# Two decoder blocks on one core: four heads' scores ahead of the expert gathers, eight ids first, and tiles moved by 32 bytes

## The chip, the core and the metric

The kernel runs on one core of a Trainium2 chip. The metric is device time in microseconds; the time before is 1990.11 us, the median of three runs (1988.2 to 1990.91). Engines are named as in the profile: PE (TensorE; PEld is its weight load), DVE (VectorE), ACT (ScalarE), POOL (GpSimd), SP (SyncE, which here only issues DMAs).

## The reference

256 tokens of width 1024 pass through two layers of a first model (each: feed-forward, mixer, feed-forward, with norms) and one layer of a second (a state-space branch and an mLSTM branch). The last part retrieves experts: for each token and each of 8 heads, 16 out of 16384 rows of two tables.

```python
q = (xb @ w_q).reshape(256, 8, 2, 128)
s = einsum('thid,hikd->thik', q, keys)            # 128 scores per half
sv, si = top_k(s, 16)                             # per half
cand = sv[..., 0, :, None] + sv[..., 1, None, :]  # 256 pairs
cs, ci = top_k(cand, 16)                          # 16 expert ids
gate = softmax(cs)
act = gelu(einsum('td,thkd->thk', xb, u_tab[eidx]))
y = einsum('thk,thkd->td', gate * act, v_tab[eidx])
out = rmsnorm(x + y, final_norm)
```

## The kernel before

**Dense part.** Every large product is computed in three passes with values split into a high and a low part (`split`, `split_scaled`): `whi`/`wlo` for the weights, `xp` (and `hh`/`hl`, `yh`/`yl`, ...) for the activations. `weights` loads a block of 1 MB (or 704 KB) into `raw` over SP's queue; `split_piece` makes `whi` on ACT and `wlo` on DVE. `acc` then issues, for each 128 rows, three matmuls of 256 columns with the weights stationary and the activations moving (L170, L171, L172); `accn` (the values `v` of the two attention mixers) has the roles the other way round (L180 to L182). The four feed-forward layers hold 4 x (11 x 2 x 48 + 8 x 66) = 6336 such matmuls; in all 9384 matmuls of 256 columns are built, 336 of them for the heads 1 to 7 of the last part.

**Tiles.** Tiles lie in pools one behind the other: `const`, `keep`, `act` and `tmp` from the bottom up, the dense weights (`wp`) from the top down. A tile takes a multiple of 32 bytes of each partition. All activations begin 32 bytes past a multiple of 64, and so do the weights. `eps2` (L52, one float, 32 bytes) lies in `const`, below nearly everything.

**Expert part** (`peer`). `score` projects a head (48 matmuls `pq`, as above), copies it to `pqT`, and multiplies by the keys (`psc`); from head 1 on the scores are copied to SBUF (`psb`). `route` turns 128 + 128 scores per token into 16 ids and gates, all on DVE: `top16` twice, 256 pairs (`cand`), `top16` again, then two one-hot products (`oh`) that look the ids up; the last is L1150. `tokens` makes the transposed tokens `hn` and the normed `xn`. `expert` (L1246) gathers one row of 8 KB per token (u and v side by side, 1 MB in all) with an indirect DMA from POOL. For every gathered tile DVE computes a dot product (L1264); two at a time ACT makes the gelu and a diagonal matrix `dg`, and PE adds `dg` times v into four banks `acc` (L1276). Only then is the tile `uv` free; there are 7 + 3 of them (`LATE`, `MORE`). There are 256 gathers: 8 heads x 2 halves of the tokens x 16. While head h is gathered, head h + 1 is scored and routed.

A scheduler orders each engine's instructions; `issue_after` holds an instruction behind another one. POOL issues the gathers in the program's order, SP its loads likewise.

**The end.** DVE adds the last expert into `hn`, adds `acc` (L1286), ACT sums the squares (L1287), DVE scales by the norm and the gain `gf` (L1293), and SP stores.

Of the kernel before, what the change touches and what calls it, by code (L numbers as in the profile page):

```python
# [17 lines left out]
T = 256  # L18
# [5 lines left out]
LATE, MORE = 7, 3  # L24
# [7 lines left out]
class Net:  # L32
    def __init__(self, ctx, tc, a):
        self.tc, self.nc, self.a, self.ctx = tc, tc.nc, a, ctx
        nc = self.nc
        self.const = ctx.enter_context(tc.tile_pool(name="const", bufs=1))
        self.keep = ctx.enter_context(tc.tile_pool(name="keep", bufs=1))
        self.dense = ExitStack()
        self.act = self.dense.enter_context(tc.tile_pool(name="act", bufs=1))
        self.tmp = self.dense.enter_context(tc.tile_pool(name="tmp", bufs=2))  # L40
        self.weighed = ExitStack()
        self.wp = self.weighed.enter_context(tc.tile_pool(name="wp", bufs=3, side="right"))
        self.dram = ctx.enter_context(tc.tile_pool(name="dram", bufs=1, space=bass.MemoryType.DRAM))
# [1080 lines left out]
    def route(self, s, r, out):  # L1124

        nc, v = self.nc, self.nc.vector
        pk = self.late.tile([128, 18, 16], F32, tag="route", name="route", bufs=6)
        two = lambda i: pk[:, i:i + 2, :]
        sv, si, ab, abf, sif, e = two(0), two(2).bitcast(U32), two(4).bitcast(U32), two(6), two(8), two(10)
        cs, ci, ids, gate = pk[:, 12, :], pk[:, 13, :].bitcast(U32), pk[:, 14, :].bitcast(I32), pk[:, 15, :]  # L1130
        out.append((ids, gate, pk[:, 16, :], pk[:, 17, :]))
        wide = lambda name: self.late.tile([128, 16, 16], F32, tag="wide", name=name, bufs=4)
        sc = wide("rsc").rearrange("p a b -> p (a b)")
        for j in range(2):
            yield from self.top16(sv[:, j], si[:, j], s[:, j], sc[:, 0:128])
        cand = wide("cand")
        yield v.tensor_tensor(cand, sv[:, 0].unsqueeze(2).to_broadcast([128, 16, 16]),
                              sv[:, 1].unsqueeze(1).to_broadcast([128, 16, 16]), OP.add)
        yield from self.top16(cs, ci, cand.rearrange("p a b -> p (a b)"), sc)
        v.tensor_scalar(ab[:, 0], ci, 4, None, op0=OP.logical_shift_right)  # L1140
        yield v.tensor_scalar(ab[:, 1], ci, 15, None, op0=OP.bitwise_and)
        v.tensor_copy(abf, ab)
        yield v.tensor_copy(sif, si)
        for j in range(2):
            oh = wide("oh")
            yield v.tensor_tensor(oh, abf[:, j].unsqueeze(2).to_broadcast([128, 16, 16]),
                                  self.iota16.unsqueeze(1).to_broadcast([128, 16, 16]), OP.is_equal)
            yield v.tensor_tensor(oh, oh, sif[:, j].unsqueeze(1).to_broadcast([128, 16, 16]), OP.mult)
            yield v.tensor_reduce(e[:, j], oh, axis=mybir.AxisListType.X, op=OP.add)
        self.routed = v.scalar_tensor_tensor(ids, e[:, 0], 128.0, e[:, 1], op0=OP.mult, op1=OP.add).ins  # L1150
# [7 lines left out]
    def peer(self, st, x, out):  # L1158
# [6 lines left out]
        for t, n in ((gn, "peer_g"), (gf, "out_g")):  # L1165
            nc.sync.dma_start(t, a[n].partition_broadcast(128))
# [4 lines left out]
        def tokens(i):  # L1171
# [6 lines left out]
            nc.vector.scalar_tensor_tensor(xn[i], hn[i], self.rcol(st)[:, i:i + 1], gn, op0=OP.mult, op1=OP.mult)  # L1178

        def score(hd, got):  # L1180
# [16 lines left out]
            if hd > 0:  # L1197
                kept = late.tile([128, 2, 256], F32, tag="psb", name="psb", bufs=2)
                for i in range(2):
                    nc.scalar.activation(kept[:, i], banks[i], AF.Copy)  # L1200
                banks = [kept[:, i] for i in range(2)]
            got += banks
            self.latest = (copied,)
            yield

        def routes(hd, out):

            s = []
            yield from score(hd, s)
            for i in range(2):  # L1210
                steps = self.route(s[i].rearrange("p (j k) -> p j k", j=2), lambda: self.rcol(st)[:, i:i + 1], out)
# [4 lines left out]
                with ExitStack() as ctx:  # L1216
# [3 lines left out]
                    while self.routed is first:  # L1220
                        next(steps)
                with self.tc.issue_after(self.routed):
                    for _ in steps:
                        pass
                if i == 0:
                    ids = self.routed
                with self.tc.issue_after(ids):
                    tokens(i)

        rt = []  # L1230
# [19 lines left out]
        for hd in range(8):  # L1250
            here, rt = rt, []
            ahead = routes(hd + 1, rt) if hd < 7 else iter(())
            for i in range(2):
# [3 lines left out]
                for k0, k1 in zip(cuts, cuts[1:]):  # L1257
                    uv = {}
                    for k in range(k0, k1):
# [4 lines left out]
                        nc.vector.scalar_tensor_tensor(u, u, 1.0, xn[i], op0=OP.mult, op1=OP.mult, accum_out=dots[:, k:k + 1])  # L1264
# [3 lines left out]
                    for k in range(k0, k1):  # L1268
                        vt = uv[k][:, D:]
                        if hd == 7 and k >= 13 and k % 2 == 1:  # L1270
                            nc.vector.scalar_tensor_tensor(hn[i], vt, w[:, k:k + 1], hn[i], op0=OP.mult, op1=OP.add)
                            continue
                        dg = late.tile([128, 128], F32, tag="dg", name="dg", bufs=8)
                        nc.scalar.activation(dg, self.ident, AF.Copy, scale=w[:, k:k + 1])  # L1274
                        for b in range(2):
                            nc.tensor.matmul(acc[i][b], dg, vt[:, b * 512:(b + 1) * 512], start=hd == 0 and k == 0,  # L1276
# [4 lines left out]
        for i in range(2):  # L1281
            z = late.tile([128, 4], F32, tag="z4", name="z4", bufs=2)
            sq = late.tile([128, 512], F32, tag="osq", name="osq", bufs=2)
# [7 lines left out]
            for b in range(2):  # L1291
                c = slice(b * 512, (b + 1) * 512)
                nc.vector.scalar_tensor_tensor(hn[i][:, c], hn[i][:, c], z[:, 3:4], gf[:, c], op0=OP.mult, op1=OP.mult)  # L1293
                nc.sync.dma_start(out[i * 128:(i + 1) * 128, c], hn[i][:, c])
# [130 lines left out]
```

## Time and profile before

| | |
|---|---|
| median of three runs | 1990.11 us |
| the profiled execution | 1995.88 us |
| its span, first to last instruction | 1994.1 us |
| PE busy | 1806.1 us (91%) |
| DVE busy | 1351.1 us (68%) |
| ACT busy | 852.6 us (43%) |
| bytes read from HBM | 488.8 MB, of them 268.45 MB by the gathers |

A matmul's busy time overlaps that of the next, so its cost in a stream is the distance from one start to the next (the pitch). The span falls into two parts: to about 1300 us the dense part, then the expert part.

### The profile page before, as it was taken

The page shows a single profiled execution, that of the slowest core. Times are in us where ns is not written, and L with a number is a line of the kernel's source. Part 1 is how long each engine was busy: PE and PEld are TensorE (multiplying, and loading weights), DVE is VectorE, ACT ScalarE, POOL GpSimd, SP SyncE. Part 2 cuts the span into 40 slices and gives each one's busy share as a digit, 9 for nine tenths or more (in the row PEclk, how much of TensorE's full clock was granted, in tenths as well). Part 3 has the DMA queues.
Part 4 walks back from the last instruction along what each step waited for, and adds up shares of the span by engine and source line. Part 5 has one row for each costly group of instructions (what it writes and reads, how often), then busy time and mean ns, then how long its engine had stood idle before and what let it go on. Part 6 is the DMA issues. An engine that isn't in the chain of part 4 may idle for free.

```text
span 1994.1 us, 31435 instructions
## 1 busy us (share of the span) xinstructions
PE 1806.1 (91%) x12097; PEld 1457.0 (73%) x12097; DVE 1351.1 (68%) x2490; ACT 852.6 (43%) x1391; POOL 605.8 (30%) x831
## 2 busy tenths in 40 slices
PE   8999899999999999999999999979988787777776
PEld 7999899999999998899997699855643333222222
DVE  6765677875675567675676376789866766665556
ACT  5544645554544466554444465444422322221112
POOL 5002212141240100200235851244344344443342
PEclk9999999999999999999999799979999899999998
DMA  5556425555554553264464125479899999999996
GB/s 209 195 175 206 149 88 184 197 188 188 195 180 163 194 179 128 98 239 169 155 223 144 43 88 177 175 304 421 360 409 421 420 422 421 421 421 421 422 421 285
DMA packets 81022, 493.30 MB, mean 247 GB/s; under 512 B 14389, under 2 KB 16693, under 8 KB 28393
## 3 DMA queue, kind: packets, MB, share of 16 engines
q0 software_dynamic: 36864, 268.45, 32.5%
q1 hardware_dynamic: 36616, 219.79, 31.6%
q10 hardware_dynamic: 7392, 3.05, 0.8%
q8 instruction: 96, 1.57, 0.3%
q14 instruction: 54, 0.43, 0.1%
HBM read 488.80 MB, written 2.13 MB: 246 GB/s over the span
## 4 chain that ended last, share of the span: by engine, by line
PE 55%; DMA 19%; DVE 14%; issue 5%; ACT 4%; POOL 3%; another core or an unknown queue 0%; DVEq 0%; SPq 0%; POOLq 0%; ACTq 0%
DMA uv<-in_peer_uv,route 15%; DVE uv L1264 4%; PE up L172 4%; PE up L171 4%; PE gate L172 4%; PE gate L170 4%; PE up L170 4%; PE gate L171 4%; PE o L170 4%; PE o L171 3%; PE o L172 3%; PE acc L1276 3%; DVE wlo L186 2%; ACT whi L185 2%; PE ip L172 1%
## 5 line engine op out<-in xcount | busy, mean ns | idle before, releaser
L186 DVE TENSOR_TENSOR wlo<-raw,whi 128x1024 fp32r<-128x1024 f32 (+3 forms) x451 | 512.3, 1151 | 192.2 <-ACT whi L185 180.9
L1276 PE MATMUL acc<-uv,dg 128*128 128x512 f32 x1008 | 484.1, 629 | 131.2 <-ACT dg L1274 131.1
L185 ACT ACTIVATE whi<-raw 128x1024 fp32r<-128x1024 f32 (+3 forms) x451 | 424.7, 964 | 345.7 <-PE gate L171 75.4
L1276 PEld LDWEIGHTS acc<-uv,dg 128*128 128x128 f32 x1008 | 191.8, 199 | 410.1 <-ACT dg L1274 208.0
L1264 DVE SCALAR_TENSOR_TENSOR uv<-uv,xn 128x1024 f32<-128x1024 f32 x256 | 311.3, 1221 | 149.5 <-DMA uv<-in_peer_uv,route 144.2
L1246 POOL DMA_INDIRECT uv<-in_peer_uv,route x256 | 282.1, 1102 | 387.1 <-PE acc L1276 237.3
L170 PE MATMUL gate<-xp,whi 128*128 128x256 f32 x704 | 199.0, 283 | 7.1 <-ACT whi L185 7.1
L172 PE MATMUL gate<-xp,wlo 128*128 128x256 f32 x704 | 197.9, 281 | 3.7 <-DVE wlo L186 3.7
L171 PE MATMUL gate<-xp,whi 128*128 128x256 f32 x704 | 197.4, 280 | 0.0
L172 PE MATMUL o<-hh,wlo 128*128 128x256 f32 x704 | 194.4, 276 | 0.5 <-DVE wlo L186 0.5
L172 PE MATMUL up<-xp,wlo 128*128 128x256 f32 x704 | 194.6, 276 | 0.0
L170 PE MATMUL up<-xp,whi 128*128 128x256 f32 x704 | 194.6, 276 | 0.0
L171 PE MATMUL up<-xp,whi 128*128 128x256 f32 x704 | 194.6, 276 | 0.0
L170 PE MATMUL o<-hh,whi 128*128 128x256 f32 x704 | 194.4, 276 | 0.0
L171 PE MATMUL o<-hl,whi 128*128 128x256 f32 x704 | 194.3, 276 | 0.0
L1266 ACT ACTIVATE route<-route 128x2 f32<-128x2 f32 x129 | 26.2, 203 | 387.7 <-DVE uv L1264 386.6
L170 PEld LDWEIGHTS gate<-xp,whi 128*128 128x128 f32 x704 | 135.0, 192 | 8.1 <-ACT whi L185 7.4
L172 PEld LDWEIGHTS gate<-xp,wlo 128*128 128x128 f32 x704 | 134.5, 191 | 5.0 <-DVE wlo L186 5.0
L171 PEld LDWEIGHTS gate<-xp,whi 128*128 128x128 f32 x704 | 134.9, 192 | 0.2
L172 PEld LDWEIGHTS o<-hh,wlo 128*128 128x128 f32 x704 | 132.2, 188 | 0.7 <-DVE wlo L186 0.7
L170 PEld LDWEIGHTS up<-xp,whi 128*128 128x128 f32 x704 | 132.4, 188 | 0.0
L170 PEld LDWEIGHTS o<-hh,whi 128*128 128x128 f32 x704 | 132.2, 188 | 0.1
(437 smaller groups left out, 3754.4 us busy)
## 6 DMA issues: line engine op xcount, KB each, us to landing
raw<-in_ffn_w_up SPq DMA_DIRECT2D x44, 1024.0 KB, 4.8
raw<-in_ffn_w_down SPq DMA_DIRECT2D x64, 704.0 KB, 4.2
raw<-in_ffn_w_gate SPq DMA_DIRECT2D x43, 1024.0 KB, 4.8
raw<-in_w_in SPq DMA_DIRECT2D x18, 1024.0 KB, 4.8
raw<-in_gla_in SPq DMA_DIRECT2D x12, 1024.0 KB, 4.8
raw<-in_sb_in SPq DMA_DIRECT2D x12, 1024.0 KB, 4.8
raw<-in_peer_q SPq DMA_DIRECT2D x8, 1024.0 KB, 8.9
raw<-in_gla_w_out SPq DMA_DIRECT2D x4, 1024.0 KB, 5.5
```

The costliest lines, as they stand in the source:

```text
L170: nc.tensor.matmul(ps, hi, xh, start=start and n == 0, stop=False)
L171: nc.tensor.matmul(ps, hi, xl, start=False, stop=False)
L172: nc.tensor.matmul(ps, lo, xh, start=False, stop=stop and n == len(steps) - 1)
L185: return (self.nc.scalar.activation(h, src, AF.Copy).ins, self.nc.vector.tensor_tensor(l, src, h.bitcast(F32), OP.subtract).ins)
L186: self.nc.vector.tensor_tensor(l, src, h.bitcast(F32), OP.subtract).ins)
L1246: nc.gpsimd.indirect_dma_start(out=t, out_offset=None, in_=a["peer_uv"], in_offset=bass.IndirectOffsetOnAxis(ap=ids[:, k:k + 1], axis=0))
L1264: nc.vector.scalar_tensor_tensor(u, u, 1.0, xn[i], op0=OP.mult, op1=OP.mult, accum_out=dots[:, k:k + 1])
L1266: gelu = nc.scalar.activation(w[:, ks], dots[:, ks], AF.Gelu_apprx_tanh).ins
L1276: nc.tensor.matmul(acc[i][b], dg, vt[:, b * 512:(b + 1) * 512], start=hd == 0 and k == 0, stop=hd == 7 and k == 14)
```

## The change

1. `eps2` is taken from a tile of nine floats, which takes 64 bytes where one float took 32: every tile of `keep`, `act`, `tmp` and most of `const` moves up by 32 bytes and now begins at a multiple of 64. The weights `whi` and `wlo` stay 32 bytes off. The gathered tiles stay 32 bytes off as well.
2. Heads 1 to 4 are scored right behind head 0 (`AHEAD = 4`), ahead of the first gather's use. The gain `gf` is loaded behind them.
3. For head 0 and the first half of the tokens, `route` takes the first 8 ids from the best 8 of each half (64 pairs; no pair outside them can be among the best 8), and the other 8 ids after that.
4. `rcol_alone` takes the column of norms from the square root's output without the row's reciprocal.
5. There are 8 + 3 gathered tiles, 6 `dg` tiles in place of 8, 14 rows in a `route` tile in place of 18.
6. `hn` enters `acc` by four matmuls with the identity. The last expert of each half adds onto `acc` directly; the 14th goes through PE like the others. At the end `gf` is multiplied in before the norm is known, and ACT scales one half.

```diff
-LATE, MORE = 7, 3
+LATE, MORE = 8, 3
+AHEAD = 4
...
-        self.eps2 = c.tile([128, 1], F32, name="eps2")
+        self.eps2 = c.tile([128, 9], F32, name="eps2")[:, 0:1]
...
+    def rcol_alone(self, st):
+
+        nc = self.nc
+        if st.rc is None:
+            r = self.keep.tile([128, T], F32, tag="rs", name="rs", bufs=1)
+            st.sqrt = nc.scalar.activation(r, self.mean_squares(st.squares), AF.Sqrt, bias=self.eps).ins
+            p = self.bank([128, 2])
+            for i in range(2):
+                nc.tensor.matmul(p[:, i:i + 1], r[0:1, i * 128:(i + 1) * 128], self.one1, start=True, stop=True)
+            st.rc = self.const.tile([128, 2], F32, name="rcol")
+            nc.vector.reciprocal(st.rc, p)
+        return st.rc
...
+        if soon:
+            for _ in range(2):
+                for j in range(2):
+                    yield next(steps[j])
+            low = slice(0, 8)
+            v.tensor_copy(sif[:, :, low], si[:, :, low])
+            some = self.wide("some", 8, 8)
+            yield v.tensor_tensor(some, *pairs(8), OP.add)
+            yield v.max(cs[:, low], flat(some))
+            cl = self.late.tile([128, 8], U32, tag="cl", name="cl", bufs=1)
+            yield v.max_index(cl, cs[:, low], flat(some))
+            yield from self.chosen(e[:, :, low], cl, sif[:, :, low], 8, 8)
+            self.routed = join(low)
+            yield
+            done = 8
...
-                kept = late.tile([128, 2, 256], F32, tag="psb", name="psb", bufs=2)
+                kept = late.tile([128, 2, 256], F32, tag="psb", name="psb", bufs=AHEAD)
...
-            self.latest = (copied,)
+            self.latest = (copied,) if hd > AHEAD else (self.ids0,) if hd else self.latest
...
+        for hd in range(1, 1 + AHEAD):
+            scored[hd] = []
+            for _ in score(hd, scored[hd]):
+                pass
+        nc.sync.dma_start(gf, a["out_g"].partition_broadcast(128))
...
+        for i in range(2):
+            for b in range(2):
+                nc.tensor.matmul(acc[i][b], self.ident, hn[i][:, b * 512:(b + 1) * 512], start=True, stop=False)
...
-                        nc.vector.scalar_tensor_tensor(u, u, 1.0, xn[i], op0=OP.mult, op1=OP.mult, accum_out=dots[:, k:k + 1])
+                        with self.tc.issue_after(self.rest0):
+                            nc.vector.scalar_tensor_tensor(u, u, 1.0, xn[i], op0=OP.mult, op1=OP.mult, accum_out=dots[:, k:k + 1])
...
-                        if hd == 7 and k >= 13 and k % 2 == 1:
-                            nc.vector.scalar_tensor_tensor(hn[i], vt, w[:, k:k + 1], hn[i], op0=OP.mult, op1=OP.add)
+                        if hd == 7 and k == 15:
+                            for b in range(2):
+                                c = slice(b * 512, (b + 1) * 512)
+                                nc.vector.scalar_tensor_tensor(hn[i][:, c], vt[:, c], w[:, k:k + 1], acc[i][b], op0=OP.mult, op1=OP.add)
...
-                nc.vector.tensor_tensor(hn[i][:, c], hn[i][:, c], acc[i][b], OP.add)
-                nc.scalar.activation(sq, hn[i][:, c], AF.Square, accum_out=z[:, b:b + 1])
+                nc.scalar.activation(xn[i][:, c], hn[i][:, c], AF.Square, accum_out=z[:, b:b + 1])
+            nc.vector.tensor_tensor(gn, hn[i], gf, OP.mult)
```

How the instructions move is shown at three places. Up to head 0's scores every engine but SP, ACT and DVE (two splits of head 1) has the same instructions in the same order.

On DVE, the end of the way from head 0's scores to the first ids, before (`cand` holds the 256 pairs, `rsc` the same without the best eight, `oh` the one-hot products, `wlo` is a weight split of head 1; the last row makes the ids of 16 experts):

```order
L1119 MAX_INDEX route<-route,cand 128x8
L1120 MATCH_REPLACE rsc<-route,cand 128x256
L1121 MAX route<-rsc 128x8
L1122 MAX_INDEX route<-route,rsc 128x8
L1140 TENSOR_SCALAR route<-route 128x16
L1141 TENSOR_SCALAR route<-route 128x16
L1142 CAST route<-route 128x32
L1146 TENSOR_TENSOR oh<-route,iota_14954 128x256 x2
L1148 TENSOR_TENSOR oh<-oh,route 128x256 x2
L1149 TENSOR_REDUCE route<-oh 128x16 x2
L186 TENSOR_TENSOR wlo<-raw,whi 128x1024
L1150 SCALAR_TENSOR_TENSOR route<-route 128x16
```

and now the whole way from the 64 pairs (`some`) on; the row L1169 makes the ids of 8 experts:

```order
L1179 TENSOR_TENSOR some<-route 128x64
L1177 CAST route<-route 128x2x8
L1180 MAX route<-some 128x8
L1182 MAX_INDEX cl<-route,some 128x8
L1143 TENSOR_SCALAR ab<-cl 128x8
L1144 TENSOR_SCALAR ab<-cl 128x8
L1145 CAST abf<-ab 128x2x8
L1148 TENSOR_TENSOR oh<-abf,iota_14953 128x64 x2
L1150 TENSOR_TENSOR oh<-oh,route 128x64 x2
L1151 TENSOR_REDUCE route<-oh 128x8 x2
L1169 SCALAR_TENSOR_TENSOR route<-route 128x8
L1134 MATCH_REPLACE rsc<-route,psc 128x128
```

The second best eight of each half and of the pairs, and head 1's split, no longer stand ahead of the first ids.

On SP, at the same place, before (`peer_q` is a head's weights, `keys` the sub-keys, `gn` and `gf` two gains):

```order
L152 DMA raw<-in_w_out 128x2048 x4
L152 DMA raw<-in_peer_q 128x2048
L1163 DMA keys<-in_peer_keys 128x2048
L1166 DMA gn<-in_peer_g 128x1024
L1166 DMA gf<-in_out_g 128x1024
L152 DMA raw<-in_peer_q 128x2048 x7
```

and now:

```order
L153 DMA raw<-in_w_out 128x2048 x4
L153 DMA raw<-in_peer_q 128x2048 x3
L1213 DMA keys<-in_peer_keys 128x2048
L1215 DMA gn<-in_peer_g 128x1024
L153 DMA raw<-in_peer_q 128x2048
L1292 DMA gf<-in_out_g 128x1024
L153 DMA raw<-in_peer_q 128x2048 x4
```

The keys, which head 0's scores need, stand behind the weights of heads 1 and 2.

On PE, around the first use of a gathered tile, now (`acc<-hn` is the identity product, `acc<-uv` the gathered tiles):

```order
L171 MATMUL pq<-xp,whi 128x256
L172 MATMUL pq<-xp,whi 128x256
L173 MATMUL pq<-xp,wlo 128x256
L1244 MATMUL psc<-keys,pqT 128x128 x4
L1299 MATMUL acc<-hn_14955,ident 128x512 x2
L1299 MATMUL acc<-hn_14956,ident 128x512 x2
L1341 MATMUL acc<-uv,dg 128x512 x32
```

The first `acc<-uv` stands behind all matmuls of heads 1 to 4; before it stood behind head 1 and the first two matmuls of head 2.

## Rows read from the trace of the kernel before

**Rows 1.** The page: busy time, share and instructions of PE.
```profile
PE 1806.1 (91%) x12097; PEld 1457.0 (73%) x12097; DVE 1351.1 (68%) x2490; ACT 852.6 (43%) x1391; POOL 605.8 (30%) x831
```
**Rows 2.** Windows of 100 us to 1300: engines' busy time (instructions), granted clock, DMA.
```profile
100.00:200.00 100.00, 99.79 (x879) 99.53 (x878) 61.05 (x77) 45.71 (x61) 11.58 (x16) 1.00 0.56 190
...
sum 1300.00, PE 1266.98 PEld 1210.04 DVE 867.56 ACT 658.33 POOL 323.76; mean PE 97.46 PEld 93.08 DVE 66.74 ACT 50.64 POOL 24.90
```
**Rows 3.** Timeline of PE, attention projection: start, duration, engine, line, instruction.
```profile
749.18 0.28 PE L171 MATMUL qk<-xp,whi 128*128 128x256 f32 x1
...
750.88 0.28 PE L171 MATMUL qk<-xp,whi 128*128 128x256 f32 x1
```
**Rows 4.** Windows of the expert part: PE, PEld, DVE, ACT, POOL, clock, DMA share, GB/s.
```profile
1300.00:1310.00 10.00, 1.84 (x13) 1.24 (x11) 9.26 (x39) 3.54 (x4) 0.00 (x0) 0.70 0.03 9
...
1400.00:1410.00 10.00, 9.12 (x33) 5.10 (x34) 9.97 (x29) 6.82 (x13) 3.81 (x3) 1.00 0.76 282
...
1440.00:1460.00 20.00, 19.24 (x73) 10.95 (x72) 11.39 (x23) 4.54 (x16) 8.55 (x7) 1.00 0.85 329
...
1800.00:1900.00 100.00, 73.55 (x161) 28.53 (x160) 52.10 (x101) 18.00 (x60) 38.33 (x40) 1.00 1.01 421
```
**Rows 5.** Timeline of POOL: the first gather issued, and the eleventh.
```profile
1310.23 1.16 POOL L1246 DMA_INDIRECT uv<-in_peer_uv,route  x1 [13.84 <-DVE route L1150]
...
1332.92 0.95 POOL L1246 DMA_INDIRECT uv<-in_peer_uv,route  x1 [8.53 <-PE acc L1276]
```
**Rows 6.** The chain that ended last, its end: start, duration, what.
```profile
1964.58 18.73 DMA uv<-in_peer_uv,route
...
1983.40 1.25 DVE uv L1264 x2
...
1985.10 1.29 DVE hn L1271
...
1989.44 0.75 DVE hn L1293
```
**Rows 7.** Timeline of PE, values of the first mixer (activations stationary).
```profile
247.55 0.28 PE L180 MATMUL v<-whi,xp 128*128 128x256 f32 x1
...
248.49 0.28 PE L182 MATMUL v<-whi,xp 128*128 128x256 f32 x1
```
**Rows 8.** Timeline of PE, second model's input projection, 272 columns.
```profile
1046.96 0.29 PE L170 MATMUL ip<-xp,whi 128*128 128x272 f32 x1
...
1048.98 0.29 PE L171 MATMUL ip<-xp,whi 128*128 128x272 f32 x1
```
**Rows 9.** Timeline of PE, merged: plain float32 matmuls of 128 and 512 columns.
```profile
267.69 1.39 PE L371 MATMUL sc<-qt,kt 128*128 128x128 f32 x11
...
1455.85 14.00 PE L1276 MATMUL acc<-uv,dg 128*128 128x512 f32 x32
```
**Rows 10.** Timeline of DVE: head 0's scores to the first ids.
```profile
1300.40 0.30 DVE L1118 MAX8 route<-psc 128x8 f32<-128x128 f32 x1 [4.61 <-PE psc L1195]
...
1304.69 0.41 DVE L1120 MATCH_REPLACE8 rsc<-route,cand 128x256 f32<-128x256 f32 x1
...
1308.64 1.21 DVE L186 TENSOR_TENSOR wlo<-raw,whi 128x1024 fp32r<-128x1024 f32 x1
1309.77 0.17 DVE L1150 SCALAR_TENSOR_TENSOR route<-route 128x16 int32<-128x16 f32 x1
```
**Rows 11.** Timeline of ACT: a split of head 0, and its copy.
```profile
1285.11 1.04 ACT L185 ACTIVATE whi<-raw 128x1024 fp32r<-128x1024 f32 x1
...
1299.21 0.66 ACT L1190 ACTIVATE pqT<-pq 128x256 f32<-128x256 f32 x2 [3.94 <-PE pq L172]
```
**Rows 12.** Timeline of SP: two DMA issues.
```profile
1279.32 0.42 SPq L1163 DMA_DIRECT2D keys<-in_peer_keys  x1
...
1294.57 18.79 SPq L152 DMA_DIRECT2D raw<-in_peer_q  x2
```
**Rows 13.** Timeline of DVE: head 0's second weight split.
```profile
1288.79 1.23 DVE L186 TENSOR_TENSOR wlo<-raw,whi 128x1024 fp32r<-128x1024 f32 x1 [0.62 <-ACT whi L185]
```

More of the change, by code (lines that the diff above doesn't have):

```diff
@@ L1122, in top16, with chosen @@
         yield v.max_index(idx[:, 8:16], vals[:, 8:16], scratch)
-    def route(self, s, r, out):
+    def chosen(self, e, ci, si, n, m):
+        v = self.nc.vector
+        ab = self.late.tile([128, 2, 16], U32, tag="ab", name="ab", bufs=2)[:, :, :n]
+        abf = self.late.tile([128, 2, 16], F32, tag="abf", name="abf", bufs=2)[:, :, :n]
+        v.tensor_scalar(ab[:, 0], ci, m.bit_length() - 1, None, op0=OP.logical_shift_right)
+        yield v.tensor_scalar(ab[:, 1], ci, m - 1, None, op0=OP.bitwise_and)
+        yield v.tensor_copy(abf, ab)
+        for j in range(2):
+            oh = self.wide("oh", n, m)
+            yield v.tensor_tensor(oh, abf[:, j].unsqueeze(2).to_broadcast([128, n, m]),
+                                  self.iota16[:, :m].unsqueeze(1).to_broadcast([128, n, m]), OP.is_equal)
+            yield v.tensor_tensor(oh, oh, si[:, j].unsqueeze(1).to_broadcast([128, n, m]), OP.mult)
+            yield v.tensor_reduce(e[:, j], oh, axis=mybir.AxisListType.X, op=OP.add)
@@ L1126, in route, with wide @@
+    def wide(self, name, n=16, m=16):
+        t = self.late.tile([128, 256], F32, tag="wide", name=name, bufs=4)[:, :n * m]
+        return t.rearrange("p (a b) -> p a b", a=n)
+    def route(self, s, r, out, soon=False):
         nc, v = self.nc, self.nc.vector
-        pk = self.late.tile([128, 18, 16], F32, tag="route", name="route", bufs=6)
+        pk = self.late.tile([128, 14, 16], F32, tag="route", name="route", bufs=6)
         two = lambda i: pk[:, i:i + 2, :]
-        sv, si, ab, abf, sif, e = two(0), two(2).bitcast(U32), two(4).bitcast(U32), two(6), two(8), two(10)
@@ L1130, in route @@
[L1130 to L1133, printed above, removed]
-        for j in range(2):
[L1135 to L1142, printed above, removed]
-        yield v.tensor_copy(sif, si)
[L1144 to L1149, printed above, removed]
@@ L1150, in route @@
-        self.routed = v.scalar_tensor_tensor(ids, e[:, 0], 128.0, e[:, 1], op0=OP.mult, op1=OP.add).ins
+        sv, si, sif, e = two(0), two(2).bitcast(U32), two(4), two(6)
+        cs, ci, ids, gate = pk[:, 8, :], pk[:, 9, :].bitcast(U32), pk[:, 10, :].bitcast(I32), pk[:, 11, :]
+        out.append((ids, gate, pk[:, 12, :], pk[:, 13, :]))
+        flat = lambda t: t.rearrange("p a b -> p (a b)")
+        sc = flat(self.wide("rsc"))
+        pairs = lambda n: (sv[:, 0, :n].unsqueeze(2).to_broadcast([128, n, n]), sv[:, 1, :n].unsqueeze(1).to_broadcast([128, n, n]))
@@ new lines, in route @@
+        join = lambda n: v.scalar_tensor_tensor(ids[:, n], e[:, 0, n], 128.0, e[:, 1, n], op0=OP.mult, op1=OP.add).ins
+        steps = [self.top16(sv[:, j], si[:, j], s[:, j], sc[:, 0:128]) for j in range(2)]
+        done = 0
+        if soon:
+            for _ in range(2):
+                for j in range(2):
+                    yield next(steps[j])
[10 more added lines that the diff above has]
+            done = 8
@@ new lines, in route @@
+        for j in range(2):
+            yield from steps[j]
+        cand = self.wide("cand")
+        yield v.tensor_tensor(cand, *pairs(16), OP.add)
+        if soon:
+            yield v.match_replace(sc, cs[:, 0:8], flat(cand), -3.4e38)
+            yield v.max(cs[:, 8:16], sc)
+            yield v.max_index(ci[:, 8:16], cs[:, 8:16], sc)
+        else:
+            yield from self.top16(cs, ci, flat(cand), sc)
+        yield v.tensor_copy(sif, si)
+        rest = slice(done, 16)
+        yield from self.chosen(e[:, :, rest], ci[:, rest], sif, 16 - done, 16)
@@ L1164, in peer @@
         gn, gf = late.tile([128, D], F32, name="gn"), late.tile([128, D], F32, name="gf")
-        for t, n in ((gn, "peer_g"), (gf, "out_g")):
-            nc.sync.dma_start(t, a[n].partition_broadcast(128))
+        nc.sync.dma_start(gn, a["peer_g"].partition_broadcast(128))
         self.iota16 = self.const.tile([128, 16], F32, name="iota16")
@@ L1202, in score @@
             got += banks
-            self.latest = (copied,)
+            self.latest = (copied,) if hd > AHEAD else (self.ids0,) if hd else self.latest
             yield
         def routes(hd, out):
-            s = []
-            yield from score(hd, s)
+            s = scored.pop(hd, [])
+            if not s:
+                yield from score(hd, s)
             for i in range(2):
-                steps = self.route(s[i].rearrange("p (j k) -> p j k", j=2), lambda: self.rcol(st)[:, i:i + 1], out)
+                steps = self.route(s[i].rearrange("p (j k) -> p j k", j=2), lambda: self.rcol_alone(st)[:, i:i + 1], out,
+                                   hd == 0 and i == 0)
                 if hd > 0:
@@ L1221, in routes @@
                         next(steps)
+                if i == 0:
+                    here = self.ids0 = self.routed
                 with self.tc.issue_after(self.routed):
@@ L1224, in routes @@
                         pass
+                with self.tc.issue_after(here):
+                    tokens(i)
+                here = self.routed
                 if i == 0:
[L1226 to L1230, printed above, removed]
+                    self.rest0 = here
+        rt, scored = [], {}
         self.routed = None
```

15 lines of the change are left out of this document (9 added, 6 removed).

## The prediction

> **What bounds the kernel now.** I read the page's engine line first: PE is busy 1806.1 of 1994.1 us [rows 1], so it is the first suspect, but an average over two stages with different limits. The windows part them. To 1300 us PE is busy 97.46% of the time at granted clock 1.00, which is 2.4 GHz, while the DMA engines stand near half and DVE at 67% [rows 2]: nothing but PE's own rate sets this stage. The timeline of one stream gives that rate: from 749.18 to 750.88 there are 15 steps in 1.70 us, 113.3 ns from one matmul of 256 columns to the next [rows 3], which is 272 cycles for 256 columns. In the expert part the limit is another: from 1800 to 1900 the DMA share is 1.01 at 421 GB/s with PE at 74% [rows 4], so a gather of 1.05 MB takes 2.49 us and the sum of bytes sets the time. That stream starts at 1310.23 [rows 5], has lost some time by 1460 (282 GB/s in 1400 to 1410, 329 in 1440 to 1460 [rows 4]) and lands its last gather at 1964.58 + 18.73 = 1983.31. Behind it stands a serial tail of dot, gate, sums, norm and store [rows 6].
>
> So three things can be gained: pitch in the dense part, an earlier and fuller stream of gathers, and a shorter tail.
>
> **The 32 bytes.** The moved tiles are the moving operand of most dense matmuls and the stationary one of the values `v`. In the trace of before every dense pair has both operands 32 bytes past a multiple of 64, so no row shows the new case. What speaks for an effect: the pitch isn't a matter of columns alone. With the roles swapped, `v` takes (248.49 - 247.55) / 8 = 117.5 ns for the same 256 columns [rows 7], and the 272 columns of `ip` take 2.02 / 16 = 126.3 ns, 13.0 more for 16 more columns, where 6.7 would be their share of a clock of 2.4 GHz [rows 8]. Something that depends on where the operands lie costs cycles. My hypothesis, an inference from the number only: 272 is 17 x 16, and 1 KB that begins 32 bytes off a multiple of 64 touches 17 lines of 64 bytes, not 16.
>
> Bounds: below, the plain float32 matmuls, which take the columns at half rate and so leave the operand twice the time. `sc` with 128 columns in two passes takes (1.39 - 0.275) / 10 = 111.5 ns for what are 256 column-steps; `acc` takes (14.00 - 0.59) / 31 = 432.6 ns per pass, 108.2 for 256 [rows 9]. Above, 113.3 if nothing changes, and 117.5 as in `v` if the new distance of the operands is a bad one. I take 111, near `sc`, since that row has streams of the same length with the fixed cost of every matmul in it. All but the 336 matmuls of heads 1 to 7 are dense, 9384 - 336 = 9048. Gain 9048 x 2.3 ns = 20.8 us, times 0.975 for the stretches that PE does not bound: **-20.3 us** (ends -45 at 108.2 and +37 at 117.5). DVE and ACT have room for this 2%.
>
> The Trainium skill's page "TensorE: Matmul & The Clock Gate", section Back-to-back issue gap, gives 262 cycles for 256 columns, 109.2 ns. The trace has 113.3. By the page, if the shift removes all that the trace has above it, this term is 9048 x 4.1 x 0.975 = -36 us, an estimate from that page.
>
> **The first gather.** The chain from head 0's scores to the ids runs on DVE from 1300.40 to 1309.94 [rows 10]. Out of it go: the second best eight of the two halves (a replace, a max and an index each, six instructions at 0.28 to 0.30 with their loads, about 1.9 us), the second best eight of the pairs (three at 0.41 to 0.43, 1.5 us), and the split of head 1 between the last product and the ids (1.13 us from 1308.64 to 1309.77). 64 pairs in place of 256 shorten the add, max, index and six one-hot operations by about 1.3 us. Together -5.8. Against it: on ACT two splits of head 1 and 2 now stand ahead of head 0's copy `pqT` (1299.21), 1.04 us each [rows 11]; the first has room in ACT's idle 3.94 us there, the second must wait until head 0's last matmuls free its buffer and costs about 1.0. Sum **-4.8** (ends -5.8 and -2).
>
> On SP the keys stand behind the weights of heads 1 and 2. Before they were issued at 1279.32 [rows 12], 20 us early. Now the load for head 2 needs the buffer that head 0's second split frees at 1288.79 + 1.23 = 1290.02 [rows 13]; the keys go out about 1290.4, two loads of 1.05 MB take 5 us at 421 GB/s and some time on the way, so I put the landing at 1296 to 1298, an estimate, and `psc` needs them near 1299.9. I cost it at nothing: the cover is 2 to 4 us of head 0's matmuls. If it is gone, the gathers start later by what is missing, up to some 4 us.
>
> **The stream of gathers.** Before, six weight loads of 1.05 MB (heads 2 to 7) lay within the stream; with four heads ahead about four remain, plus half a MB of `gf`: 1.6 MB less at 421 GB/s, **-3.8 us**. PE is the price. The first `acc<-uv` now stands behind heads 1 to 4 (192 matmuls at 113.3, 22 us) and the identity products (4 of two passes at 432.6 ns, 3.5 us), all behind head 0: first buffer free about 1335 rather than before the eleventh gather at 1332.92, which had waited 8.53 us for `acc` [rows 5]. Eleven buffers in place of ten cover some 27 to 30 us from 1306: a hole of 0 to 3 us in the stream. To be had on the other side are the two dips, worth (1 - 282/421) x 10 + (1 - 329/421) x 20 = 7.7 us [rows 4], in which PE scored and served heads at once. DVE still has about 4 us of dots and routing per early gather where the stream brings one in 2.49. I take **-2** (ends -7 and +5).
>
> **The tail.** `hn` takes the last expert in 1.29 us, then two adds of `acc` at 0.70 and two squares [rows 6]. Now the last expert is added onto `acc` in two halves of about 0.7, the squares begin behind the first: -0.6 to -1.3. The last scale, 0.75, is shared with ACT: -0.3. `acc` must hold expert 14 by then: -0 to +0.5. **-1.3** (ends -2 and 0). Norm column, `dg` and `route` buffers: hidden by the wait for DMA, nothing.
>
> **Sum.** Expert part -4.8 - 3.8 - 2 - 1.3 = -11.9 (ends -18 and -1); with the pitch -32.2. The profiled execution took 1995.88, which stands 5.8 over the median of 1990.11, so it becomes 1963.7, and on the median's basis **1958**.
>
> **Rivals.**
> *The pitch falls all the way* to that of `acc`, 108.2 [rows 9]: -45.0 - 11.9, **1933** (at 109.2, 1942). For it: 272 cycles being an exact multiple of 16. Against: `sc` keeps 111.5 with twice the time per operand. The clock-gate page's section named above speaks for this rival, and no run of before shows its 109.2.
> *The shift does nothing*: **1978**. For it: 113.3 may be the fixed cost of a matmul with its weight load, and `v` differs by roles and not by place. Against: the odd 13 ns of `ip` [rows 8]. The Trainium skill's page "SBUF — State Buffer", section Specifications, has 16-byte cachelines, of which 32 bytes is a multiple; by that rule nothing would change. It says of start alignment that its rule is "about legality, not speed", and no row here shows both alignments.
> *The streams get in each other's way*: stationary and moving operand now differ by an odd multiple of 32 bytes, a distance that never occurred before. If all go to 117.5 as `v` does [rows 7], +37 - 12 = +25, **2015**. It decides from a pitch above 113.3 + 11.9 / (9048 x 0.975) = 114.6 ns. For it: `v` and `ip` show that distance or role costs up to 4 ns and more. Against: no row puts the loss of `v` on the distance rather than on the role.
> *The gathers gain nothing*: keys late by 4, hole 3, dips remain: the expert part stands at -1; this widens each case by 11 us upward.
>
> **How the numbers follow.** Chances: forecast 0.33, full fall 0.30, no effect of the shift 0.24, streams in each other's way 0.13. A measurement of this kernel can tell about 0.2%, 4 us, from no change. Forecast and full fall are faster under all bounds; of the third case 0.20 is faster and 0.04 within 4 us; the fourth is slower. So 0.83, 0.04 and 0.13. The range runs from the full fall with the expert part at its better end, 1933 - 7 = 1926, to the no-effect case with the expert part at its worse end and a little over, 1978 + 11 = 1989, and 3 us more for what the bounds of the rows leave open; it leaves out the fourth case, 0.13, and the far ends of the others. The forecast's own range is 1948 to 1969.
>
> **What would show it.** A stream of 256-column matmuls at 111 ns (below 109.5: the second case; 113.3: the third; above 114.6: the fourth), the same in `gate`, `qk` and `o`; `v` apart. The ids 9.5 - 5.8 us behind the first max; the first gather 4.8 us nearer to head 0's last projection matmul; the keys landed before `psc` is due. The twelfth gather's wait for `acc` below 3 us; no window under 400 GB/s between 1320 and 1460. From the last landing to the end of the scale less than the 6.9 us of before [rows 6]. I am wrong if the dense part's length changes by another sign, or if PE's idle share in it grows.

## The result, and the profile after

The changed kernel took 2014.03 us (median of six runs, 2008.84 to 2017.28) beside 1990.51 for the kernel before: a ratio of 1.0109, with a 95% interval from 1.0088 to 1.0129. It is slower by 1.1%. The forecast was 1958; of the cases worked out it is the fourth, the streams that get in each other's way (2015).

The profiled execution took 2008.84 us with a span of 2007.1. Four places part the span. The first is the dense step: on PE's timeline of the attention projection of the changed kernel (start, duration, engine, line, instruction; the rows that answer to [rows 3]) there stand 15 steps between these two rows.

```profile
741.04 0.28 PE L171 MATMUL qk<-xp,whi 128*128 128x256 f32 x1
...
742.82 0.28 PE L171 MATMUL qk<-xp,whi 128*128 128x256 f32 x1
```

They take 1.78 us: 118.7 ns a step, where it was 113.3. The second place is the way from head 0 to the first gather: PE's last projection matmul and its first scores, DVE's first max and the first ids, and POOL's gathers, the first, the ninth, the eleventh and the twelfth.

```profile
1320.52 0.27 PE L173 MATMUL pq<-xp,wlo 128*128 128x256 f32 x1
1322.15 1.16 PE L1244 MATMUL psc<-keys,pqT 128*128 128x128 f32 x8 [1.36 <-ACT pqT L1239]
```

```profile
1322.90 0.49 DVE L1132 MAX8 route<-psc 128x8 f32<-128x128 f32 x2 [2.68 <-PE psc L1244]
...
1326.09 0.17 DVE L1169 SCALAR_TENSOR_TENSOR route<-route 128x8 int32<-128x8 f32 x1
```

```profile
1327.18 1.83 POOL L1308 DMA_INDIRECT uv<-in_peer_uv,route  x1 [9.19 <-PE ht L1225]
...
1349.85 1.91 POOL L1308 DMA_INDIRECT uv<-in_peer_uv,route  x1 [11.14 <-ACT pqT L1239]
...
1356.73 1.63 POOL L1308 DMA_INDIRECT uv<-in_peer_uv,route  x1 [3.66 <-PE pq L173]
1364.71 1.15 POOL L1308 DMA_INDIRECT uv<-in_peer_uv,route  x1 [6.34 <-PE acc L1341]
```

From the first max to the first gather it is 4.28 us, where it was 1310.23 - 1300.40 = 9.83 [rows 5, 10]. The ids themselves are ready 3.36 us behind the first max (1326.09 + 0.17 - 1322.90), before 9.54; the gather follows them by 0.92 us, before by 0.29. The last place is the tail, on DVE's timeline: the last dot, the last expert onto `acc`, the product with `gf`, the scale.

```profile
1997.35 1.23 DVE L1327 SCALAR_TENSOR_TENSOR uv<-uv,xn 128x1024 f32<-128x1024 f32 x1 [0.82 <-DMA uv<-in_peer_uv,route]
...
1999.15 1.61 DVE L1336 SCALAR_TENSOR_TENSOR hn<-uv,route,acc 128x512 f32<-128x512 f32 x2
2000.80 1.23 DVE L1351 TENSOR_TENSOR gn<-hn,gf 128x1024 f32<-128x1024 f32 x1
...
2002.65 0.49 DVE L1358 TENSOR_SCALAR gn<-gn,z 128x512 f32<-128x512 f32 x1
```

The two profiled spans differ by 13.0 us, and these places account for it. For head 0's last projection matmul before, and its first scores, the same timeline has:

```profile
1298.90 0.28 PE L172 MATMUL pq<-xp,wlo 128*128 128x256 f32 x1
1299.65 1.16 PE L1195 MATMUL psc<-keys,pqT 128*128 128x128 f32 x8 [0.47 <-ACT pqT L1190]
```

| stretch | before | after | difference | forecast |
|---|---|---|---|---|
| start to head 0's last projection | 1298.90 | 1320.52 | +21.6 | -20.3 |
| from there to the first gather | 11.33 | 6.66 | -4.7 | -4.8 |
| first gather to the last dot | 673.17 | 670.17 | -3.0 | -5.8 |
| last dot to the end of the span | 10.7 | 9.75 | -0.95 | -1.3 |

The profiled executions differ by 13 and the medians by 23.5: the profiled execution of before took 5.4 us more than its median, that of after 5.2 less than its own. Most of this is a stretch at half the clock that the one of before had and the one of after had not. Here are the windows of the same stretch of the second model (columns as in [rows 4]): before, and behind it after.

```profile
1113.00:1163.00 50.00, 50.00 (x239) 37.12 (x238) 21.36 (x33) 26.08 (x45) 44.45 (x177) 0.83 0.12 43
```

```profile
1140.00:1181.60 41.60, 41.60 (x235) 32.29 (x235) 21.20 (x33) 25.62 (x45) 37.14 (x144) 1.00 0.14 52
```

PE is busy throughout in both. Before, in finer windows:

```profile
1100.00:1105.00 5.00, 3.19 (x28) 3.00 (x26) 3.93 (x8) 3.96 (x5) 4.61 (x15) 1.00 0.00 0
1105.00:1110.00 5.00, 5.00 (x18) 3.21 (x17) 3.00 (x7) 0.63 (x1) 4.61 (x12) 0.66 0.34 102
...
1115.00:1120.00 5.00, 5.00 (x29) 4.11 (x28) 1.79 (x4) 3.25 (x8) 4.45 (x20) 0.97 0.01 3
1120.00:1125.00 5.00, 5.00 (x14) 3.54 (x13) 1.14 (x3) 4.57 (x9) 4.38 (x21) 0.50 0.00 2
1125.00:1130.00 5.00, 5.00 (x13) 2.89 (x12) 0.00 (x0) 0.96 (x2) 4.38 (x21) 0.50 0.00 0
1130.00:1135.00 5.00, 5.00 (x12) 2.28 (x11) 2.21 (x3) 1.63 (x5) 4.45 (x17) 0.50 0.31 93
...
1140.00:1145.00 5.00, 5.00 (x28) 3.81 (x28) 1.54 (x4) 2.98 (x6) 4.41 (x20) 1.00 0.00 0
```

From 1120 to 1135 the granted clock is 0.50, which is 1.2 GHz. PE had stood idle for 1.8 us between 1100 and 1105, and the clock fell a first time in the 5 us behind it (0.66). Ahead of the long stretch PE was busy for 15 us without a pause and the clock was back near 1.00; what made it fall at 1120 these rows don't show. The stretch lengthens the profile of before by 50.00 - 41.60 = 8.4 us; without it the loss up to head 0's last projection would read 21.6 + 8.4 = 30.

### The profile page after: what moved, and what is told of

It reads as the page before. It is cut to its first block, busy times and chain, and to the rows that moved or that the text cites. A ratio compares the mean times of both kernels' runs of the same rounds, so it can differ in the third digit from the quotient of the medians.

```text
span 2007.1 us, 31534 instructions
## 1 busy us (share of the span) xinstructions
PE 1824.7 (91%) x12113; PEld 1482.4 (74%) x12113; DVE 1349.6 (67%) x2497; ACT 855.5 (43%) x1395; POOL 640.0 (32%) x831
## 4 chain that ended last, share of the span: by engine, by line
PE 56%; DMA 19%; DVE 13%; issue 4%; POOL 4%; ACT 3%; SPq 0%; POOLq 0%; ACTq 0%; DVEq 0%
DMA uv<-in_peer_uv,route 17%; PE o L171 5%; PE o L172 4%; DVE uv L1327 4%; PE o L173 4%; PE up L172 4%; PE up L173 4%; PE up L171 4%; PE gate L171 4%; PE gate L173 4%; PE gate L172 4%; PE acc L1341 2%; DVE wlo L187 2%; ACT whi L186 1%; PE ip L173 1%
## 5 line engine op out<-in xcount | busy, mean ns | idle before, releaser
L1308 POOL DMA_INDIRECT uv<-in_peer_uv,route x256 | 313.4, 1224 | 348.4 <-DMA uv<-in_peer_uv,route 136.9
L171 PE MATMUL gate<-xp,whi 128*128 128x256 f32 x704 | 201.8, 287 | 7.5 <-ACT whi L186 7.5
L172 PE MATMUL gate<-xp,whi 128*128 128x256 f32 x704 | 200.4, 285 | 0.0
L172 PE MATMUL up<-xp,whi 128*128 128x256 f32 x704 | 197.9, 281 | 0.0
L171 PE MATMUL up<-xp,whi 128*128 128x256 f32 x704 | 197.8, 281 | 0.0
L173 PEld LDWEIGHTS up<-xp,wlo 128*128 128x128 f32 x704 | 132.7, 188 | 0.0
```

What stands on the lines that cost most here:

```text
L171: nc.tensor.matmul(ps, hi, xh, start=start and n == 0, stop=False)
L172: nc.tensor.matmul(ps, hi, xl, start=False, stop=False)
L173: nc.tensor.matmul(ps, lo, xh, start=False, stop=stop and n == len(steps) - 1)
L1308: nc.gpsimd.indirect_dma_start(out=t, out_offset=None, in_=a["peer_uv"], in_offset=bass.IndirectOffsetOnAxis(ap=ids[:, k:k + 1], axis=0))
```

## The experiments

**Shift or expert part, and distance or alignment.** My theory behind the result: the step of a dense stream depends on the address of the stationary operand less that of the moving one, modulo 256 bytes (the *distance*). The traces hold no addresses; those used here are the ones that the built programs give their tiles. In the kernel before the distance is 64 for 8640 of the 9672 dense matmuls of 256 or 272 columns, and the shift makes it 32. The rivals: the alignment of one operand by itself, or the expert part.

e1, the kernel before with the shift alone:

```diff
-        self.eps2 = c.tile([128, 1], F32, name="eps2")
+        self.eps2 = c.tile([128, 9], F32, name="eps2")[:, 0:1]
```

> The kernel before with the 32 bytes alone (eps2 of nine floats). Distance theory: the step from one dense matmul to the next depends on the address of the stationary operand less that of the moving one, taken modulo 256 bytes; 64 gives 113.3 ns, and the shift makes it 32, which gives 118. Then the time is 1990 + 31 = about 2021 us (2015 to 2027). Alignment theory (a moving operand at a multiple of 64 bytes is itself the slower one): the same 2021 here. Third theory, the shift is innocent and the expert part costs the time: 1990.

Measured: 2020.74 us beside 1991.85, ratio 1.0144 (1.0119 to 1.0169). The shift alone costs 28.9 us, which is all of the loss and more.

e2, the changed kernel without the shift:

```diff
-        self.eps2 = c.tile([128, 9], F32, name="eps2")[:, 0:1]
+        self.eps2 = c.tile([128, 1], F32, name="eps2")
```

> The changed kernel with eps2 of one float, so all tiles lie as before. Distance and alignment theory: the dense steps are 113.3 ns again and only the expert part differs from before: 1990 - 9.5 = about 1981 us (1976 to 1986). If the expert part costs the time: 2014.

Measured: 1980.07 us, ratio 0.9949 (0.9918 to 0.998). The expert part does gain, 11.8 us by the medians (8.5 when the same kernel ran again as e10).

e3, the changed kernel with the weights moved as well:

```diff
+        self.weighed.enter_context(tc.tile_pool(name="pad", bufs=1, side="right")).tile([128, 56], F32, name="pad")
         self.wp = self.weighed.enter_context(tc.tile_pool(name="wp", bufs=3, side="right"))
```

> The changed kernel with the dense weights moved as well, down by 224 bytes: stationary and moving operand both begin at multiples of 64 bytes, and their distance is 64 modulo 256 again. Distance theory: steps of 113.3 ns, about 1981 us, as without the shift. Alignment theory: the moving operand is still at a multiple of 64, steps of 118 ns, about 2014 us. A theory of 64-byte lines (what begins at such a multiple touches 16 lines and not 17): steps near 109 ns, about 1950 us.

Measured: 1988.31 us, ratio 0.9989 (0.9972 to 1.0006). PE's timeline of its attention projection, 20 steps between the rows:

```profile
716.98 0.28 PE L172 MATMUL qk<-xp,whi 128*128 128x256 f32 x1
...
719.25 0.28 PE L174 MATMUL qk<-xp,wlo 128*128 128x256 f32 x1
```

2.27 us for 20 steps, 113.5 ns: the step of before, not 118 or 109, with both operands at multiples of 64 bytes. Alignment of the moving operand costs nothing, and 64-byte lines give nothing. By the medians it stays 8 us behind e2 and 2 behind e10, which is the same kernel as e2. Part of it may lie in the gathers: in the profiles the ninth follows the first by 29.15 us (1300.43 to 1329.58), in e2 by 25.74.

e4, the kernel before with the activations 64 bytes further:

```diff
-        self.eps2 = c.tile([128, 1], F32, name="eps2")
+        self.eps2 = c.tile([128, 17], F32, name="eps2")[:, 0:1]
```

> The kernel before with eps2 of 17 floats: the activations move by 64 bytes, so both operands begin 32 bytes off a multiple of 64 as before, and their distance is 0 modulo 256. Distance theory: steps of 117.5 to 118 ns, about 2018 us (2012 to 2026). Alignment theory: nothing changes, 113.3 ns and 1990 us.

Measured: 2035.3 us, ratio 1.0223 (1.0199 to 1.0246). Both operands are aligned as before; only the distance is another. Its timeline, 9 steps between the rows:

```profile
743.74 0.28 PE L171 MATMUL qk<-xp,whi 128*128 128x256 f32 x1
...
744.82 0.28 PE L171 MATMUL qk<-xp,whi 128*128 128x256 f32 x1
```

1.08 us for 9 steps, 120 ns, more than the 118 expected, so 17 us more than expected. Alignment theory falls here, and distance stands. e4 also parts distance from role, which the rows of before could not: the products `v`, whose stationary operand is the activations, stand at 192 in the kernel before (117.5 ns [rows 7]) and at 0 in e4, 26 steps between these rows:

```profile
250.16 0.28 PE L180 MATMUL v<-whi,xp 128*128 128x256 f32 x1
...
253.28 0.28 PE L182 MATMUL v<-whi,xp 128*128 128x256 f32 x1
```

3.12 us for 26 steps, 120.0 ns, as `qk` has at 0 with the roles the other way round. The next table has all steps between two neighbouring matmuls of 256 columns that both stand at the commonest distance of their kernel, put together from the trace and the program's addresses; steps above 140 ns, in which PE paused or ran at the lower clock, are left out.

| kernel | moving, stationary (mod 64) | distance (mod 256) | steps | mean ns | of them 115 ns or less |
|---|---|---|---|---|---|
| before | 32, 32 | 64 | 8256 | 113.9 | 7290 |
| after | 0, 32 | 32 | 8295 | 118.3 | 504 |
| e1 | 0, 32 | 32 | 8271 | 118.3 | 358 |
| e2 | 32, 32 | 64 | 8285 | 114.1 | 6968 |
| e3 | 0, 0 | 64 | 8165 | 114.1 | 6907 |
| e4 | 32, 32 | 0 | 8588 | 119.9 | 20 |

**Is 64 the best place?** e5 moves the low part of the weights only, on top of the shift:

```diff
+        self.step = (getattr(self, "step", -1) + 1) % 13
+        o = 4 * self.step
+        lo = self.wp.tile([128, 1072], F32R, tag="wlo", name="wlo", bufs=self.wbufs[1])[:, o:o + K * N].rearrange("p (k n) -> p k n", k=K)
```

> A measurement, of no use as a kernel: before with the 32 bytes, and the low weights begin at 13 offsets in turn, 0 to 192 bytes in steps of 16, so one of every three dense matmuls has its own distance from 32 to 224 modulo 256 bytes, and the trace gives the step for each. Distance theory: 113 ns or less for 64 and 117 to 120 for 32, 128, 192 and those between; distances of 48 and 80 show whether 64 is the best one, below 113 if a still better place exists. Alignment theory: the step does not follow the offset of the stationary operand, 118 throughout.

Measured: one run, 2022.1 us. The scan did not tell. By the offset, the steps had means from about 117 to 120.5 ns, and at 64 it was 118.6, whether the moving operand is paired with its own weights or with those loaded behind it. One matmul in three at 64 between two at 32 gets nothing. So the distance of a single pair isn't enough.

e8 gives whole streams one distance, both parts of a block at the same offset (and the shift of 32 again):

```diff
+        b, o = self.cut % 4, 16 * (self.cut // 4 % 5)
+        at = [(o, o), (0, 64), (128, 0), (64 + o, o)][b]
+        hi, lo = (self.wp.tile([128, 1024 + s], F32R, tag=tag, name=tag, bufs=self.wbufs[1])[:, f // 4:f // 4 + K * N].rearrange("p (k n) -> p k n", k=K)
+                  for tag, s, f in (("whi", 32, at[0]), ("wlo", 16, at[1])))
```

> A measurement, of no use as a kernel: both parts of a weight block begin at the same offset, so that whole streams of 24 matmuls have one distance of 32, 48, 64, 80, 96 or 160 modulo 256 bytes (the scan before moved one matmul in three only, and no offset stood out). Distance theory: 64 gives 113.3 ns a step in such a stream, the others 117 to 120. If a neighbour, 48 or 80, is below 113, there is a better place than that of before. If 64 gives 118 in such short streams, the step depends on more than the distance in the stream itself, on what ran ahead of it.

Measured: one run, 2025.81 us. PE's timeline shows a stream of distance 64 (first pair of rows, 20 steps) and, two blocks later, one of distance 80 (second pair, 21 steps):

```profile
395.39 0.28 PE L174 MATMUL up<-xp,whi 128*128 128x256 f32 x1
...
397.66 0.28 PE L176 MATMUL up<-xp,wlo 128*128 128x256 f32 x1
...
406.35 0.28 PE L174 MATMUL up<-xp,whi 128*128 128x256 f32 x1
...
408.84 0.28 PE L174 MATMUL up<-xp,whi 128*128 128x256 f32 x1
```

2.27 / 20 = 113.5 ns and 2.49 / 21 = 118.6 ns, 9 us apart in one run. Over all streams of 15 or more steps (a step above 140 ns ends a stream), with the mean over the streams and the least and greatest mean of one:

| distance | streams | mean ns | least | greatest |
|---|---|---|---|---|
| 32 | 18 | 118.2 | 117.7 | 118.6 |
| 48 | 18 | 118.1 | 117.7 | 118.4 |
| 64 | 18 | 115.0 | 113.5 | 117.9 |
| 80 | 19 | 118.7 | 118.5 | 119.0 |
| 96 | 18 | 118.1 | 117.1 | 118.9 |
| 160 | 48 | 119.6 | 119.0 | 120.1 |

64 is the only place of these with the short step, and 16 bytes to either side lose it. But of the 18 streams at 64 four run at 118 throughout (their median step); the other 14 have a median of 113 or 114.

The kernels whose dense matmuls stand at 64 show the same two steps, and when they change. In the kernel before, 8015 of the 8256 steps at 64 lie in 53 stretches of ten steps or more without a break (a step above 122 ns or another distance ends a stretch). In 39 of them nearly all steps take 113 to 115 ns, in 13 nearly all take 116 or more, and one is mixed. So a stretch keeps the step that it starts with until PE is interrupted: the 216 steps from 609 us on are all long, the 1510 from 27 us on nearly all short. Which of the two it is can differ between executions of one kernel. e2 and e10 are the same kernel; in their profiles this long stretch reads, e2 first (columns as in [rows 4]):

```profile
27.10:198.10 171.00, 171.00 (x1511) 171.00 (x1510) 111.93 (x133) 83.61 (x106) 14.79 (x21) 1.00 0.54 191
```

```profile
27.40:205.10 177.70, 177.70 (x1511) 177.70 (x1510) 112.48 (x133) 83.87 (x106) 14.89 (x21) 1.00 0.54 185
```

The same 1511 matmuls at the same clock take 171.0 and 177.7 us, 113.2 and 117.6 ns each. That is 6.7 of the 8.1 us by which the two profiled executions differ (1976.13 and 1984.24). So 64 allows the short step and does not force it, and how many stretches miss it is a part of the spread between executions; what decides at the start of a stretch was not found.

**The expert part.** e6 scores two heads ahead:

```diff
-AHEAD = 4
+AHEAD = 2
```

> The changed kernel without the shift, with two heads scored ahead and not four. Theory: the ninth gather waits (14.29 us) since its buffer lies where the dense weights lay, which the last of the heads ahead sets free; with two heads it is issued some 10 us earlier after the first gather and the hole in the stream (252 GB/s between 1320 and 1325, some 4 us in all) goes, while two more loads of 1.05 MB fall into the stream (5 us): 1980 + 1 = about 1981 us (1977 to 1986), the first release of a buffer for the twelfth gather 10 us nearer to the first gather. Rival, the second eight ids are what is late: the ninth gather stays where it is, and the time is 1985.

Measured: 1982.65 us, ratio 0.9945 (0.9924 to 0.9966). POOL's timelines tell more than the time: the first, eighth, ninth and twelfth gathers with four heads ahead (e2),

```profile
1295.31 1.83 POOL L1308 DMA_INDIRECT uv<-in_peer_uv,route  x1 [9.09 <-DVE route L1135]
...
1305.83 0.94 POOL L1308 DMA_INDIRECT uv<-in_peer_uv,route  x1 [0.30 <-DVE route L1169]
1321.05 0.99 POOL L1308 DMA_INDIRECT uv<-in_peer_uv,route  x1 [14.29 <-ACT pqT L1239]
...
1334.68 1.10 POOL L1308 DMA_INDIRECT uv<-in_peer_uv,route  x1 [5.89 <-DVE oh L1148]
```

and with two (e6):

```profile
1300.72 1.84 POOL L1308 DMA_INDIRECT uv<-in_peer_uv,route  x1 [9.09 <-DVE route L1135]
...
1311.40 0.94 POOL L1308 DMA_INDIRECT uv<-in_peer_uv,route  x1 [0.31 <-issue]
1312.64 0.93 POOL L1308 DMA_INDIRECT uv<-in_peer_uv,route  x1 [0.30 <-issue]
...
1329.00 0.94 POOL L1308 DMA_INDIRECT uv<-in_peer_uv,route  x1 [11.92 <-DVE route L1169]
```

The ninth gather's wait of 14.29 us is gone with two. In e2 the second eight ids were made at 1305.54 on DVE, 15 us before that gather, so ids were not what it waited for: the last three buffers lie where the dense weights lay, and heads 1 to 4 still use that place. The windows of e2 show the hole, and those of e6 at the same times show none:

```profile
1320.00:1325.00 5.00, 4.47 (x39) 4.27 (x38) 5.00 (x19) 4.39 (x13) 1.92 (x2) 1.00 0.73 252
1325.00:1330.00 5.00, 4.47 (x34) 3.79 (x33) 5.00 (x17) 3.21 (x8) 1.07 (x1) 1.00 0.92 365
1330.00:1335.00 5.00, 5.00 (x13) 2.23 (x12) 5.00 (x24) 2.46 (x4) 0.32 (x1) 1.00 0.85 338
1335.00:1340.00 5.00, 5.00 (x13) 2.27 (x12) 5.00 (x21) 3.60 (x8) 3.44 (x4) 1.00 0.73 256
```

```profile
1320.00:1325.00 5.00, 0.85 (x3) 0.56 (x3) 1.80 (x7) 2.40 (x4) 0.00 (x0) 0.54 1.02 424
1325.00:1330.00 5.00, 5.00 (x6) 2.11 (x7) 4.69 (x16) 3.33 (x10) 0.94 (x1) 0.50 1.01 421
```

e6 keeps above 400 GB/s from 1305 to 1375 and has its dip later, 156 GB/s from 1375 to 1380. By their times e6 and e2 can't be told apart (ratios 0.9945 and 0.9949), so that the two loads that return into the stream take back what the hole cost agrees with the runs and is not shown by them.

e7 takes the sixteen ids at once:

```diff
                 steps = self.route(s[i].rearrange("p (j k) -> p j k", j=2), lambda: self.rcol_alone(st)[:, i:i + 1], out,
-                                   hd == 0 and i == 0)
+                                   False)
```

> The changed kernel without the shift, where head 0's first ids come from the usual way of sixteen. By the sum the first gather comes 4 to 5 us later behind the first max, and the time is 1980 + 4 = about 1984 us (1982 to 1987). If the ninth gather's wait is what bounds the start of the stream, and it does not depend on the first ids, the time stays at 1980.

Measured: 1991.33 us over ten runs that spread from 1982.6 to 1999.5, ratio 0.9996 (0.9974 to 1.0017). That is 11 more than e2 by the medians and, by the ratios, 7 to 9 more than e10 and e2, not 4. The profile has the step itself near its expected size: the first max at 1294.61, the first gather at 1304.07, 9.46 us, and 4.27 in e2. The rest isn't in this place; the first max alone came 3.6 us later than in e2. About 3 us of that goes with the granted clock, an estimate from the windows of the two profiles (0.89 against 0.94 from 900 to 930, 0.91 against 1.00 from 1210 to 1230). What the other executions lost I don't settle.

e9 scores three heads ahead (`AHEAD = 3`), e10 is e2 again beside it.

> The changed kernel without the shift, with three heads scored ahead: between four (1980.1) and two (1982.7). The ninth gather waits about 6 us less than the 14.29 with four, one load of 1.05 MB more (2.5 us) lies in the stream: 1980 us (1977 to 1984).

> The changed kernel without the shift once more, in five rounds beside the kernel before, to place it: 1980 us, 0.5% under the kernel before.

Measured: e9 1977.44 us, ratio 0.992 (0.9903 to 0.9938); e10 1985.96, ratio 0.9962 (0.9944 to 0.998), beside 1994.5 for the kernel before. Three ahead has the lowest median of all kernels here, 0.8% under the kernel before. Beside four ahead in the same rounds (e10) the intervals of the ratios don't meet; beside two ahead (0.9924 to 0.9966) they overlap. In e9's timeline the ninth gather waited 9.05 us and followed the first by 20.52, about the time that eight gathers take (8 x 2.49 = 19.9), so hardly a hole is left.

## Why the prediction was wrong, point by point

- **What bounds the kernel: right.** PE's rate set the dense stage and the stream of gathers the rest. The time went where the step went.
- **The 32 bytes: this step failed.** It read "I take 111, near `sc`". The measured step is 118.3 ns in the mean, 4.4 above the 113.9 of before and not 2.3 below 113.3, and the term of -20.3 us came out near +30. The hypothesis under it, 17 lines of 64 bytes, is refuted by e3, where both operands begin at multiples of 64 and the step is still 113.5. The rows that were on the table pointed elsewhere: `v` and `ip` [rows 7, 8] are slower with the same alignment as `qk` [rows 3], so alignment could not be what parted them. Their distances, 192 for `v`, were to be had from the operands' places, and none but 64 had the short step; that it is the distance and not the role, only e4 showed. I wrote of this as "a distance that never occurred before" and gave it 0.13; the rows gave 113.3 for one distance and 117.5 and more for another, with no distance better than 64, so this case deserved a larger chance.
- **The fourth case: right that the distance counts, its time partly luck.** It gave +37 for the dense part and 2015 in all; alone the shift cost 28.9 (e1), and the whole came to 2014. The condition, a step above 114.6, was met. But the dense term was 8 us too large and the expert part gained 8.65 in place of 11.9, and the one error hides a part of the other. What 37 had too much lies in part in the 1032 dense matmuls at other distances, slow already, and in the 966 of the 8256 steps at 64 that took more than 115 ns in the profile of before. And its reason, "an odd multiple of 32 bytes", is not the rule: the distance of 0 in e4 is slower still.
- **The Trainium skill's pages.** The Trainium skill's page "TensorE: Matmul & The Clock Gate", section Back-to-back issue gap, has 262 cycles (109.2 ns) for 256 columns, for a matmul by itself, and says that in a stream the weight loads set the spacing too; the short step of the streams here is 113.3 to 114.0. The Trainium skill's page "SBUF — State Buffer", section Specifications, has lines of 16 bytes, from which the prediction took a rule by which 32 bytes would change nothing; e1 shows 4.4 ns a step from 32 bytes.
- **The first gather: right.** -4.7 against -4.8: -5.55 from the first max to the gather, and +0.88 ahead of it, on ACT (2.38 us from the last projection matmul to the first max, 1.50 before). On DVE the ids came 6.18 us sooner behind the first max, where 5.8 was forecast; 0.63 of that was lost between the ids and the gather, a wait that the prediction did not have (in e2 the gather's row names DVE's L1135, an instruction behind the ids). The keys were no wait: `psc` waited for `pqT`, so their cover held.
- **The stream: right in sign, half its size.** -3.0 against -5.8. What I had missed is the place of the last three buffers. The 27 to 30 us that the prediction gave to eleven buffers shrink to the cover of eight, some 20. The twelfth gather still waited 6.34 us for `acc`, where under 3 was forecast, and a window of 270 GB/s stands between 1360 and 1370:

```profile
1360.00:1370.00 10.00, 10.00 (x25) 4.50 (x24) 10.00 (x44) 7.20 (x14) 3.55 (x4) 1.00 0.76 270
```

- **The tail: right.** -0.95 against -1.3. Of it 0.74 lies between the last dot and the scale (2002.65 - 1997.35 = 5.30 us, 6.04 before [rows 6]) and 0.21 behind the scale. `acc` was a wait of 0.1 us: the second half of the last expert starts 0.11 us behind the end of the first, just after PE's last product.

## What to carry to other kernels

Where PE bounds a stage, the steps of its matmuls can be worth more than a rearrangement: 4.4 ns in each of some 8300 outweighed all that the expert part gained here. Before a change that moves tiles, even by one scalar's 32 bytes, work out from the addresses of stationary and moving operand which distance each stream has, and read the step of each distance from the trace: a kernel that has been tuned by trial may sit at a good one without saying so. When two executions of one kernel differ, compare the windows over the same matmuls: a whole stretch can have run at another step. When buffers reuse a region, ask who leaves that region last, not how many buffers there are.

## What the runs showed of the hardware

Two operands in different tiles, each well aligned, cost 4 to 6 ns a step more or less by their distance modulo 256 bytes. The means were 113.9 ns at 64, 118.3 at 32 and 119.9 at 0 over whole kernels, and 118.1 at 48 and 118.7 at 80 over the streams of e8. This holds for streams: a single matmul at 64 among others gains nothing (e5). At 64 both steps occur, 113 and 118 ns, and a stretch keeps the one that it starts with: 1511 matmuls took 171.0 us in one execution of a kernel and 177.7 in another, at the same granted clock (e2, e10). Why 64, and what decides at a stretch's start, no run here tells.
